# Block 0 of a decoder layer: gates and branch outputs with features on the partitions, and a last projection of split parts

## The chip, the cores and the metric

The kernel runs on one core of a Trainium2 chip. A core has five engines that run their own instruction streams and meet at semaphores: TensorE (PE in the profile; its weight loads are listed as PEld), VectorE (DVE), ScalarE (ACT), GpSimd (POOL) and SyncE (SP, which here issues most transfers). A matmul has a stationary operand, loaded into the array by a weight load (at most 128 x 128), and a moving operand whose columns stream through; its result goes to a bank of PSUM, from which DVE and ACT read.

The metric is the device time of one execution in microseconds. Lower is better.

## What is computed

One decoder layer over 512 tokens with 1024 features. A normalised input goes through one wide projection, three token mixers use parts of it, and each mixer's output is projected, weighted by a gate of its own for every channel, and summed. The sum goes through one more projection and is added to the input. A retrieval layer of 16384 single-neuron experts follows.

```python
h = rmsnorm(x, norm1_g[l])
z = h @ w_in[l]
...
gates = jax.nn.sigmoid((gl + b_gate[l]).astype(jnp.float32)).astype(x.dtype)
gates = gates.reshape(B, S, N_BRANCH, D)
merged = (gates[:, :, 0] * (o_fox @ w_fox_o[l])
          + gates[:, :, 1] * (o_swa @ w_swa_o[l])
          + gates[:, :, 2] * (o_mem @ w_mem_o[l]))
x = x + merged @ w_out[l]
x = x + peer_ffn(rmsnorm(x, norm2_g[l]), w_peer_q[l], peer_keys1[l], peer_keys2[l],
                 peer_u[l], peer_v[l])
```

The change touches the lines from `gates` to `x + merged @ w_out`, for the first 128 tokens only.

## The kernel before

The 512 tokens are four blocks of 128. `GROUPS` (L25) makes two groups of them: block 0 alone, and blocks 1 to 3 together. `mixers(g, hT)` (L623) runs for block 0, then for the other three. When block 0 is through, the search for its experts (`beside`, L904) is emitted in small pieces between the work of the second group; later stages treat the experts of all blocks.

**Split parts.** Most products are made of three. A 32-bit number is split into a high part, rounded to the type that the profile calls fp32r, and the low rest. `mm3` (L143) adds high x high, high x low and low x high into one bank. A weight matrix arrives by DMA in a `raw` tile of 512 KB; `load` (L115) casts it to `whi` on ACT, and `rest` (L122) subtracts to get `wlo`, for block 0 on DVE. There are three slots each for `whi` and `wlo`, and for `raw` three and, during block 0, five more. A few products are made of plain 32-bit numbers in one matmul instruction, for which the trace lists two passes, each with its own weight load.

**Two orientations.** With tokens on the partitions, the block's activations stand in the array and 256 columns of weights move (`gemm_nat`, L283). With features on the partitions, 128 x 128 pieces of weights stand and the group's tokens move (`gemm_tr`, L322): 384 columns for the second group.

**Block 0's gates** (`gates`, L581; called once for each mixer). For each of four pairs of 128-feature chunks, `gemm_nat` makes a [128 tokens, 256 features] result with 24 products. A gate's bias then differs along the columns, so ACT spreads the pair's bias values into a diagonal matrix each (L588), and a plain product of a matrix of ones with them (L300) adds the bias to every token. ACT's tanh (L591) writes a `g` tile; there are `KC` = 8 slots of these. The second group takes `gemm_tr` (L594): there the bias is one number for each partition and goes into the tanh instruction.

**Branch outputs** (`branch`, L599). For each of the four 256-column groups of a mixer's output projection, 12 products of split parts; DVE multiplies by gate + 1 and adds to `merged` (L602, L604, L605). Block 0's `merged` has tokens on its partitions.

**Last projection** (from L651). The projection needs features on the partitions, so block 0's `merged` is turned by eight transposes on PE (L656) and copied with the factor 0.5 by ACT (L658). `gemm_plain` (L303) multiplies it by raw, unsplit weights (L315), four times 8 products of 256 columns. DVE adds the input x (L673), which SP has loaded into freed `g` slots (L670), and ACT takes squares for the next norm (L209). The second group's `merged` has features on its partitions already; it is split (L661, L662) and goes through `gemm_nat`.

**Order.** In the part up to the second group's search a scheduler sets each engine's order ahead of time, by the program's order, priorities and a model of time; it is fixed in the compiled kernel. Each engine then works strictly in that order. The input rows of the second group are fetched and normalised (`get_x`, L940) among block 0's last gates and branch.

Of the kernel before, what the change touches and what calls it, by code (L numbers as in the profile page):

```python
# [7 lines left out]
F32 = mybir.dt.float32  # L8
F32R = mybir.dt.float32r
# [48 lines left out]
def tile_block(ctx: ExitStack, tc: tile.TileContext, t: dict, out: bass.AP):  # L58
# [15 lines left out]
    def bank(tag):  # L74
        return (mixed if BANKS[tag] == 1 else psum).tile([128, 512], F32, tag=tag, name=tag, bufs=BANKS[tag])
# [171 lines left out]
    for hf in range(2):  # L247
        squares(xg[:, 0, hf * 512:(hf + 1) * 512], xsum[:, 0, hf:hf + 1])
    nc.sync.dma_start(cst[:, 1:], t["c_mats"][:, 1:])
    hT = [chunks(by_k(x)) for x in (ep.tile([128, D], F32R, tag="own", name="own"),  # L250
                                    pp.tile([128, D], F32R, name="ownlo", bufs=1))]
    norm_t([xg[:, 0]], xsum, g1, *hT, tags=("tp", "sc", "tp", "sc", "tg", "acc", "mm", "tp"))

    identb = consts.tile([128, 128], BF16, name="identb")
# [25 lines left out]
        for h in range(8):  # L280
            tc.keep_in_program_order(A.mul(slope[:, h], ident, 2.0 ** -(h + 1)))

    def gemm_nat(lhs, src, n, nb, use, more=None, fetch=None, cast=None):  # L283

        w = [load_split(src[half], 4, n, fetch=fetch, cast=cast) for half in range(2)]
        for b in range(nb):
            ps = bank("mm")[:, :n]
            tok = slice(b * 128, (b + 1) * 128)
            if cast:
                for i, (lt, rt) in enumerate(((0, 0), (0, 1), (1, 0))):  # L290
                    for dc in range(KC):
                        PE.matmul(ps, lhs[lt][dc][:, tok], w[dc // 4][rt][:, dc % 4],
                                  start=i == dc == 0, stop=i == 2 and dc == KC - 1)
                use(b, ps)
                continue
            for dc in range(KC):
                wh, wl = (x[:, dc % 4] for x in w[dc // 4])
                mm3(ps, (lhs[0][dc][:, tok], lhs[1][dc][:, tok]), (wh, wl), dc == 0, dc == KC - 1 and not more)
            if more:
                PE.matmul(ps, ones, more, start=False, stop=True)  # L300
            use(b, ps)

    def gemm_plain(lhs, src, n, use, fetch):  # L303

        ps = bank("mm")[:, :n]
        for half in range(2):
            pump()
            raw = fetch(src[half], 4 * n)
            if len(src[half].shape) == 3:
                w = raw[:, :4 * n].rearrange("p (c k w) -> p k c w", c=src[half].shape[0], k=4)  # L310
            else:
                w = raw[:, :4 * n].rearrange("p (k w) -> p k w", k=4)
            for k in range(4):
                dc = 4 * half + k
                PE.matmul(ps, lhs[dc], w[:, k], start=dc == 0, stop=dc == KC - 1)  # L315
        use(0, ps)

    def halves(two):

        return two[:, :, :512], two[:, :, 512:]  # L320

    def gemm_tr(h, src):  # L322

# [257 lines left out]
    def gates(g, i, hT, ccs=range(4)):  # L581
        gs = []
        for cc in ccs:
            c0 = 8 * i + 2 * cc
            if len(GROUPS[g]) == 1:
                bias = pp.tile([128, 256], F32, tag="sq", name="bias")
                for c in range(2):
                    A.activation(bias[:, c * 128:(c + 1) * 128], ident, AF.Copy, scale=hb[:, c0 + c:c0 + c + 1])  # L588
                gs.append(new_g(256))
                gemm_nat(hT, halves(t["w_tr"][c0:c0 + 2]), 256, 1,  # L590
                         lambda b, ps: A.activation(gs[-1], ps, AF.Tanh, scale=0.5), more=bias)  # L591
                continue
            for c in range(2):
                ps = gemm_tr(hT, t["w_tr"][c0 + c])  # L594
                gs.append(new_g(ps.shape[1]))
# [3 lines left out]
    def branch(grp, i, merged, oT, gs):  # L599
# [6 lines left out]

        for cc in range(4):
            wo = load_split(t["w_o"][4 * i + cc], 4, 256)
            if len(GROUPS[grp]) == 1:
                ps = bank("mm")[:, :256]  # L610
                for kc in range(4):
                    mm3(ps, (oT[0][:, kc, :], oT[1][:, kc, :]), (wo[0][:, kc], wo[1][:, kc]), kc == 0, kc == 3)
                gated(merged[:, cc * 256:(cc + 1) * 256], gs[cc], ps)
                continue
            for c in range(2):
                ps = bank("mm")[:, :oT[0].shape[2]]
                cols = slice(c * 128, c * 128 + 128)
# [5 lines left out]
    def mixers(g, hT):  # L623
# [24 lines left out]
            get_x()  # L648
        branch(g, 2, merged, oT, gs)

        mT = [by_k(ep.tile([128, D], F32, tag="own", name="own"))] if nb == 1 else pair(nb)  # L651
        if nb == 1:
            for q in range(2):
                ps = bank("tp")
                for i in range(4):
                    PE.transpose(ps[:, i * 128:(i + 1) * 128], merged[:, (4 * q + i) * 128:(4 * q + i + 1) * 128], ident)  # L656
                ps, dst = ps.rearrange("p (k s) -> p k s", k=4), slice(4 * q, 4 * q + 4)
                A.activation(mT[0][:, dst], ps, AF.Copy, scale=0.5)  # L658
        else:
            for ct, src in enumerate(chunks(by_k(merged))):  # L660
                A.activation(mT[0][:, ct], src, AF.Copy, scale=0.5)  # L661
                V.scalar_tensor_tensor(mT[1][:, ct], src, 0.5, mT[0][:, ct].bitcast(F32),  # L662
                                       op0=OP.mult, op1=OP.subtract)
        mT = [chunks(x) for x in mT]
        x1, sums = by_token(wide(f"mg{g}", nb)), new_sums(4)
        for c in range(4):
# [6 lines left out]
                V.tensor_add(x1[:, b, cols], xs[b], ps)  # L673
                squares(x1[:, b, cols], sums[:, b, c:c + 1])

            if nb == 1:
                gemm_plain(mT[0], t["w_out"][c], 256, use, load_raw)
            else:
                gemm_nat(mT, t["w_out"][c], 256, nb, use)
        return x1, sums  # L680


# [674 lines left out]
```

## Time and profile before

| What | us |
|---|---|
| median of 3 runs | 1583.12 (1581.81 to 1583.77) |
| the profiled execution, as timed | 1584.12 |
| its span, first to last instruction | 1582.3 |
| block 0's gates, branches and projection, by the timeline | about 73 to 184 |
| of that: bias products (L300), 24 passes, recorded | 7.1 |
| of that: bias copies (L588), 24 on ACT | 8.3 |
| of that: plain products of the last projection (L315), 64 passes, recorded | 14.5 |

How to read the rows that follow. A row of the view by groups has line, engine, operation, the names of output and inputs, shapes and count; then busy time in us and the mean of one in ns; then the idle time just before them and what ended it. A row of the timeline has start and duration in us, engine, line, operation, names, shape and the number of instructions that were merged into the row. A row for one tile has the minimum, median and maximum of the durations in ns. A recorded matmul includes its way through the array, so successive ones overlap: from one start to the next is what a product costs in a stream. A shape such as 128x256 is partitions x columns; the moving operand's columns are what is shown for a matmul.

### The profile page before, as it was taken

How to read it: one execution, taken by the hardware profiler on the slowest of the kernel's cores; microseconds unless marked ns; L12 is line 12 of the kernel's file. 1: busy time of each engine (PE TensorE's matmuls, PEld its weight loads, DVE VectorE, ACT ScalarE, POOL GpSimd, SP SyncE). 2: the span in 40 equal slices, each digit the busy share in tenths (PEclk: the TensorE clock that was granted, in tenths of full speed). 3: DMA queues.
4: the chain of work that ended last, by engine and by line, in shares of the span. 5: the costliest groups of instructions: out<-in, count | busy, mean ns of one | idle time of the engine just before them, and what ended most of it. 6: DMA issues, size and time to landing. Idle time of an engine off the chain costs nothing.

```text
span 1582.3 us, 27174 instructions
## 1 busy us (share of the span) xinstructions
PE 1512.7 (96%) x9458; PEld 1373.8 (87%) x9458; DVE 1422.0 (90%) x2661; ACT 819.9 (52%) x1831; POOL 789.2 (50%) x643
## 2 busy tenths in 40 slices
PE   8999899999999989999998999899999999999998
PEld 7989899998898989898787898688888888888887
DVE  6678487888999999999899999799999999999997
ACT  7778336646345533452215998554454454444442
POOL 1100015767576456977444665445555554555451
PEclk9999999999999999999999999999999999999999
DMA  8677657898998899987798999999999999999995
GB/s 319 212 252 251 236 197 251 307 368 310 326 348 309 280 342 337 321 307 250 240 401 303 375 396 386 347 399 390 408 409 409 410 410 407 408 406 404 408 409 193
DMA packets 178361, 531.90 MB, mean 336 GB/s; under 512 B 17456, under 2 KB 46384, under 8 KB 178224
## 3 DMA queue, kind: packets, MB, share of 16 engines
q0 software_dynamic: 73728, 268.47, 44.9%
q1 hardware_dynamic: 94416, 225.95, 39.3%
q10 hardware_dynamic: 10080, 35.75, 5.7%
q8 instruction: 74, 1.21, 0.3%
q14 instruction: 63, 0.52, 0.1%
HBM read 515.42 MB, written 14.68 MB: 335 GB/s over the span
## 4 chain that ended last, share of the span: by engine, by line
PE 58%; DVE 14%; issue 10%; DMA 10%; POOL 5%; ACT 2%; POOLq 0%; SPq 0%; DVEq 0%; ACTq 0%
PE mm L1029 9%; PE mm L146 9%; PE mm L145 9%; PE mm L147 9%; DMA row<-in_peer_v_dram,eidx 6%; POOL row L868 5%; PE sc L1104 3%; DVE two L896 2%; DVE wlo L131 2%; DMA row<-in_peer_u_dram,eidx 2%; PE sc L147 2%; PE sc L146 2%; PE tp L145 2%; PE tp L146 2%; PE sc L145 2%
## 5 line engine op out<-in xcount | busy, mean ns | idle before, releaser
L868 POOL DMA_INDIRECT row<-in_peer_v_dram,eidx x256 | 328.9, 1285 | 289.2 <-DVE two L896 164.1
L868 POOL DMA_INDIRECT row<-in_peer_u_dram,eidx x256 | 316.9, 1238 | 236.3 <-DVE scr L883 115.4
L131 DVE TENSOR_TENSOR wlo<-raw,whi 128x1024 fp32r<-128x1024 f32 (+1 forms) x228 | 278.1, 1221 | 34.2 <-ACT whi L119 30.0
L896 DVE SCALAR_TENSOR_TENSOR two<-row,acts,two 128x1024 f32<-128x1024 f32 x189 | 242.5, 1283 | 4.1 <-DMA row<-in_peer_v_dram,eidx 1.9
L119 ACT CAST whi<-raw 128x1024 fp32r<-128x1024 f32 x146 | 152.6, 1050 | 105.6 <-PE mm L146 59.7
L883 DVE SCALAR_TENSOR_TENSOR scr<-row,own 128x1024 bf16<-128x1024 f32 x128 | 156.2, 1220 | 19.0 <-DMA row<-in_peer_u_dram,eidx 17.9
L883 DVE SCALAR_TENSOR_TENSOR scr<-row,two 128x1024 bf16<-128x1024 f32 x116 | 140.9, 1215 | 5.1 <-DMA row<-in_peer_u_dram,eidx 4.3
L203 POOL TENSOR_TENSOR rsy<-rsv,mhalf 128x4 f32<-128x4 f32 (+5 forms) x25 | 38.6, 1546 | 185.6 <-DVE rsv L202 184.2
L1157 ACT CAST ah<-ga 128x256 fp32r<-128x256 f32 x116 | 47.0, 407 | 158.1 <-PE tp L146 123.8
L147 PE MATMUL mm<-hhi,wlo 128*128 128x384 f32 x320 | 110.6, 346 | 4.5 <-POOL wlo L129 4.5
L145 PE MATMUL mm<-hhi,whi 128*128 128x384 f32 x320 | 111.5, 348 | 1.6 <-ACT hhi L237 1.2
L146 PE MATMUL mm<-hlo,whi 128*128 128x384 f32 x320 | 111.9, 350 | 0.0
L1159 ACT CAST whi<-raw 128x1024 fp32r<-128x1024 f32 x96 | 100.3, 1047 | 16.1 <-DMA raw<-in_peer_v_dram 11.4
L146 PE MATMUL sc<-wlo,ah 128*128 128x512 f32 x256 | 101.2, 395 | 6.3 <-DVE wlo L131 6.3
L145 PE MATMUL mm<-whi,hhi 128*128 128x256 f32 (+1 forms) x360 | 103.7, 290 | 2.9 <-DVE g L604 1.9
L146 PE MATMUL mm<-wlo,hhi 128*128 128x256 f32 (+1 forms) x360 | 102.6, 286 | 1.5 <-DVE wlo L131 1.5
L147 PE MATMUL mm<-whi,hlo 128*128 128x256 f32 (+1 forms) x360 | 101.9, 285 | 0.8 <-DVE hlo L662 0.8
L147 PE MATMUL sc<-whi,al 128*128 128x512 f32 x256 | 101.6, 397 | 0.0
L145 PE MATMUL tp<-whi,ah 128*128 128x512 f32 x256 | 101.0, 395 | 0.0
L145 PE MATMUL sc<-whi,ah 128*128 128x512 f32 x256 | 101.0, 395 | 0.0
L146 PE MATMUL tp<-wlo,ah 128*128 128x512 f32 x256 | 100.9, 394 | 0.0
L147 PE MATMUL tp<-whi,al 128*128 128x512 f32 x256 | 100.6, 393 | 0.0
(323 smaller groups left out, 4527.8 us busy)
## 6 DMA issues: line engine op xcount, KB each, us to landing
raw<-in_peer_v_dram SPq DMA_DIRECT2D x96, 512.0 KB
hhi<-in_uT_dram ACTq DMA_DIRECT2D x68, 512.0 KB
raw<-in_w_tr_dram SPq DMA_DIRECT2D x48, 512.0 KB
raw<-in_w_nat_dram SPq DMA_DIRECT2D x40, 512.0 KB
last<-in_peer_v_dram SPq DMA_DIRECT2D x32, 512.0 KB
hhi<-in_uT_dram SPq DMA_DIRECT2D x26, 512.0 KB
raw<-in_w_o_dram SPq DMA_DIRECT2D x24, 512.0 KB
gd<-st SPq DMA_DIRECT2D x24, 512.0 KB
```

What stands on the lines that cost most here:

```text
L119: (cast or A.copy)(hi[:, :n * w], raw[:, :n * w])
L131: V.tensor_sub(lo, raw, hi.bitcast(F32))
L145: PE.matmul(ps, lh, rh, start=first, stop=False)
L146: PE.matmul(ps, lh, rl, start=False, stop=False)
L147: PE.matmul(ps, ll, rh, start=False, stop=last)
L868: G.indirect_dma_start(out=r, out_offset=None, in_=t["peer_" + tab], in_offset=bass.IndirectOffsetOnAxis(ap=eidx[b][:, j:j + 1], axis=0))
L883: V.scalar_tensor_tensor(scr, r, 1.0, two[0] if b else h2n[b], op0=OP.mult, op1=OP.mult, accum_out=acts[b][:, c]))
L896: V.scalar_tensor_tensor(two[0], r, acts[b][:, c], two[0], op0=OP.mult, op1=OP.add))
L1029: PE.matmul(ps[:, :TD], w[:, dc], h2f[dc], start=dc == 0, stop=dc == KC - 1)
L1104: PE.matmul(ps[:, u], o[:, 1, u], o[:, 0, u], start=True, stop=True)
L1157: A.copy(ah, a)
L1159: A.copy(hi, raw)
```

## The change

For block 0, the gates and the branch outputs take the way that the second group takes.

- `gates` calls `gemm_tr` for every 128-feature chunk: weights stand, block 0's 128 tokens move. The bias goes into the tanh. The bias copies, the product with ones and the parameter `more` are gone.
- `branch` makes two results of 128 features with 12 products each from a loaded piece of weights, and two sets of DVE operations.
- `merged` then has features on the partitions; the transposes are gone. Each of its eight chunks is copied with 0.5 by ACT into the high part and subtracted on DVE for the low part. The low part takes the tile that held the low part of block 0's input (`ownlo`).
- The last projection calls `gemm_nat`: its weights are split like all others (eight casts on ACT, eight subtractions on DVE), with 24 products for each 256 columns. `gemm_plain` and `halves` are gone.

```diff
-                                    pp.tile([128, D], F32R, name="ownlo", bufs=1))]
+                                    pp.tile([128, D], F32R, tag="ownlo", name="ownlo", bufs=1))]
...
-    def gemm_nat(lhs, src, n, nb, use, more=None, fetch=None, cast=None):
+    def gemm_nat(lhs, src, n, nb, use, fetch=None, cast=None):
...
-                mm3(ps, (lhs[0][dc][:, tok], lhs[1][dc][:, tok]), (wh, wl), dc == 0, dc == KC - 1 and not more)
-            if more:
-                PE.matmul(ps, ones, more, start=False, stop=True)
+                mm3(ps, (lhs[0][dc][:, tok], lhs[1][dc][:, tok]), (wh, wl), dc == 0, dc == KC - 1)
             use(b, ps)
-
-    def gemm_plain(lhs, src, n, use, fetch):
...
-    def halves(two):
...
             c0 = 8 * i + 2 * cc
-            if len(GROUPS[g]) == 1:
-                bias = pp.tile([128, 256], F32, tag="sq", name="bias")
-                for c in range(2):
-                    A.activation(bias[:, c * 128:(c + 1) * 128], ident, AF.Copy, scale=hb[:, c0 + c:c0 + c + 1])
-                gs.append(new_g(256))
-                gemm_nat(hT, halves(t["w_tr"][c0:c0 + 2]), 256, 1,
-                         lambda b, ps: A.activation(gs[-1], ps, AF.Tanh, scale=0.5), more=bias)
-                continue
             for c in range(2):
                 ps = gemm_tr(hT, t["w_tr"][c0 + c])
...
             wo = load_split(t["w_o"][4 * i + cc], 4, 256)
-            if len(GROUPS[grp]) == 1:
-                ps = bank("mm")[:, :256]
-                for kc in range(4):
-                    mm3(ps, (oT[0][:, kc, :], oT[1][:, kc, :]), (wo[0][:, kc], wo[1][:, kc]), kc == 0, kc == 3)
-                gated(merged[:, cc * 256:(cc + 1) * 256], gs[cc], ps)
-                continue
             for c in range(2):
                 ps = bank("mm")[:, :oT[0].shape[2]]
...
-        mT = [by_k(ep.tile([128, D], F32, tag="own", name="own"))] if nb == 1 else pair(nb)
-        if nb == 1:
-            for q in range(2):
-                ps = bank("tp")
-                for i in range(4):
-                    PE.transpose(ps[:, i * 128:(i + 1) * 128], merged[:, (4 * q + i) * 128:(4 * q + i + 1) * 128], ident)
-                ps, dst = ps.rearrange("p (k s) -> p k s", k=4), slice(4 * q, 4 * q + 4)
-                A.activation(mT[0][:, dst], ps, AF.Copy, scale=0.5)
-        else:
-            for ct, src in enumerate(chunks(by_k(merged))):
-                A.activation(mT[0][:, ct], src, AF.Copy, scale=0.5)
-                V.scalar_tensor_tensor(mT[1][:, ct], src, 0.5, mT[0][:, ct].bitcast(F32),
-                                       op0=OP.mult, op1=OP.subtract)
+        mT = pair(nb) if nb > 1 else [by_k(ep.tile([128, D], F32R, tag="own", name="own")),
+                                      by_k(pp.tile([128, D], F32R, tag="ownlo", name="ownlo", bufs=1))]
+        for ct, src in enumerate(chunks(by_k(merged))):
+            A.activation(mT[0][:, ct], src, AF.Copy, scale=0.5)
+            V.scalar_tensor_tensor(mT[1][:, ct], src, 0.5, mT[0][:, ct].bitcast(F32),
+                                   op0=OP.mult, op1=OP.subtract)
...
-            if nb == 1:
-                gemm_plain(mT[0], t["w_out"][c], 256, use, load_raw)
-            else:
-                gemm_nat(mT, t["w_out"][c], 256, nb, use)
+            gemm_nat(mT, t["w_out"][c], 256, nb, use)
```

More of the change, by code (lines that the diff above doesn't have):

```diff
@@ L297, in gemm_nat @@
                 wh, wl = (x[:, dc % 4] for x in w[dc // 4])
-                mm3(ps, (lhs[0][dc][:, tok], lhs[1][dc][:, tok]), (wh, wl), dc == 0, dc == KC - 1 and not more)
-            if more:
-                PE.matmul(ps, ones, more, start=False, stop=True)
+                mm3(ps, (lhs[0][dc][:, tok], lhs[1][dc][:, tok]), (wh, wl), dc == 0, dc == KC - 1)
             use(b, ps)
-    def gemm_plain(lhs, src, n, use, fetch):
[L305 to L310, printed above, removed]
-            else:
[L312 to L316, printed above, removed]
-    def halves(two):
-        return two[:, :, :512], two[:, :, 512:]
     def gemm_tr(h, src):
@@ L674, in use @@
                 squares(x1[:, b, cols], sums[:, b, c:c + 1])
-            if nb == 1:
-                gemm_plain(mT[0], t["w_out"][c], 256, use, load_raw)
-            else:
-                gemm_nat(mT, t["w_out"][c], 256, nb, use)
+            gemm_nat(mT, t["w_out"][c], 256, nb, use)
         return x1, sums
```

## The prediction

> **What bounds the kernel now.** I read the page's first and fourth parts, then the busy time by stretch, then the order of time on PE in the part that the change touches. The page first: PE is the busiest engine and has most of the chain that ended last.
>
> ```profile
> PE 1512.7 (96%) x9458; PEld 1373.8 (87%) x9458; DVE 1422.0 (90%) x2661; ACT 819.9 (52%) x1831; POOL 789.2 (50%) x643
> ...
> PE 58%; DVE 14%; issue 10%; DMA 10%; POOL 5%; ACT 2%; POOLq 0%; SPq 0%; DVEq 0%; ACTq 0%
> ```
>
> All that changes belongs to block 0: its gates, its branch outputs and its last projection. By the timeline they lie between 73 and 184 us. The view by stretch (us, busy of PE, PEld, DVE, ACT, POOL with instruction counts, granted clock, DMA share, GB/s) says:
>
> ```profile
> 73.00:100.00 27.00, 24.71 (x204) 23.68 (x203) 20.58 (x33) 22.64 (x49) 6.05 (x4) 1.00 0.83 290
> 100.00:133.00 33.00, 32.60 (x252) 30.04 (x251) 25.95 (x46) 26.20 (x59) 0.69 (x1) 1.00 0.73 239
> 133.00:166.60 33.60, 33.60 (x277) 33.06 (x276) 28.32 (x44) 24.34 (x45) 1.51 (x2) 1.00 0.81 251
> 166.60:183.60 17.00, 15.85 (x80) 13.57 (x79) 2.51 (x6) 3.23 (x10) 0.00 (x0) 1.00 0.52 180
> 183.60:563.00 379.40, 365.87 (x2544) 340.71 (x2543) 333.51 (x757) 193.17 (x484) 218.42 (x190) 0.99 0.85 300
> ```
>
> From 73 to 166.6 us PE is idle 2.7 of 93.6 us; DVE is busy 74.9, ACT 73.2, and DMA has about a fifth free. The granted clock is 1.00 (the 2.4 GHz level). So **PE is the bound here**, and what its instructions gain or lose shows in full, unless DVE catches up. A recorded matmul overlaps its neighbours, so I price PE by steps from start to start, not by durations. Between 166.6 and 183.6 us (the last projection) PE works alone. Behind it PE stays busy 366 of 379 us, and the choice of experts for block 0 waits for this result, so I see no later slack that swallows a shift: what block 0 costs more, the end comes later.
>
> **What a step on PE costs.** From the timeline of PE: first and last of 14 successive products of split parts with 256 columns, then of 18 with 384, then of 9 with 512.
>
> ```profile
> 161.25 0.28 PE L146 MATMUL mm<-wlo,ohi 128*128 128x256 f32 x1
> ...
> 162.78 0.28 PE L147 MATMUL mm<-whi,olo 128*128 128x256 f32 x1
> 308.24 0.34 PE L146 MATMUL mm<-hlo,whi 128*128 128x384 f32 x1
> ...
> 311.23 0.34 PE L145 MATMUL mm<-hhi,whi 128*128 128x384 f32 x1
> 1302.14 0.39 PE L145 MATMUL sc<-whi,ah 128*128 128x512 f32 x1
> ...
> 1304.00 0.39 PE L147 MATMUL tp<-whi,al 128*128 128x512 f32 x1
> ```
>
> The steps are 1.53/13 = 0.118 us, 2.99/17 = 0.176 and 1.86/8 = 0.232: some 0.057 us for every 128 columns. Continued to 128 columns that would be 0.060 us. The change makes the products of gates and branch outputs 128 columns wide (one block's tokens move, weights stand), and twice as many. **No row here shows a split product with 128 columns**, so its step has to be bounded. The nearest rows are plain 32-bit ones: 128 columns (each product is two passes with a load each, and the 16 are passes), 64 columns, and their weight loads.
>
> ```profile
> 191.16 1.95 PE L746 MATMUL mm<-aT,raw 128*128 128x128 f32 x16
> 277.21 1.00 PE L502 MATMUL acc<-v,pT 128*128 128x64 f32 x8
> L146 PEld LDWEIGHTS mm<-wlo,hhi 128*128 128x128 f32 x360 | 68.6, 191 | 3.7 <-issue 1.9 <-DVE wlo L131 1.7
> L502 PEld LDWEIGHTS acc<-v,pT 128*128 128x128 f32 x160 | 20.4, 191 | 1.7 <-issue 1.1 <-ACT p L499 0.3 <-ACT qn L352 0.2
> L373 PEld LDWEIGHTS tp<-cst,p 128*128 128x128 f32 x168 | 20.6, 145 | 2.5 <-issue 1.3 <-ACT p L499 0.3
> ```
>
> A pass with 128 columns steps at (1.95 − 0.28)/15 = 0.112 us. A pass with 64 columns steps at (1.00 − 0.28)/7 = 0.104, though it has half the columns to move. So the columns don't set that step; the load before each pass does. A split product's load is recorded as 191 ns, just as long as the plain pass's 191, while a transpose's takes 145: loads of split parts look like those of plain numbers. With 256 columns the load hides under 0.118 us; with 128 it wouldn't. I take **0.112 us**. Bounds: 0.060 (the line, loads hidden) below, 0.224 (a plain 128-column product, two passes) above.
>
> The Trainium skill (TensorE: Matmul & The Clock Gate, Back-to-back issue gap) gives 81 ns for each load-and-matmul pair at 128 columns in a sustained stream, and 131 ns at 512; by its 81 ns the forecast would be about 1594 us. This trace has 232 ns at 512 columns, so it doesn't bear that pair of figures out for these numbers.
>
> **The change part by part.**
>
> *Gates* (12 pairs of chunks). Before: 24 products of 256 columns and one plain bias product, in two passes, per pair.
>
> ```profile
> 157.40 0.59 PE L300 MATMUL mm<-bias,cst 128*128 128x256 f32 x2
> 157.84 1.05 PE L236 MATMUL sc<-dg,mg 128*128 128x128 f32 x8
> L588 ACT ACTIVATE bias<-cst,hb 128x128 f32<-128x128 f32 x24 | 8.3, 400 | 0.0
> L591 ACT ACTIVATE g<-mm 128x256 f32<-128x256 f32 x12 | 4.6, 381 | 0.0
> ```
>
> The bias passes take 157.84 − 157.40 = 0.44 us a pair. So 288 × 0.118 + 12 × 0.44 = 39.2 us now. After: 576 × 0.112 = 64.5. That is **+25.3 us**. ACT loses the 24 bias copies (8.3 us) and writes 24 narrow gates in place of 12; it isn't the bound. The loads keep their number and size (24 of 512 KB), and the rows that SP fetches only get longer.
>
> *Branch outputs* (12 pairs). 144 × 0.118 = 16.9 us becomes 288 × 0.112 = 32.3: **+15.4 us**. DVE's multiply-adds go from one of 256 columns to two of 128:
>
> ```profile
> L131 DVE TENSOR_TENSOR wlo<-raw,whi 128x1024 fp32r<-128x1024 f32 x43 | 52.4, 1223 | 12.9 <-ACT whi L119 12.8
> L605 DVE TENSOR_TENSOR mg<-mg,g 128x256 f32<-128x256 f32 x7 | 2.9, 420 | 0.1
> L604 DVE SCALAR_TENSOR_TENSOR g<-g,mm 128x256 f32<-128x256 f32 x7 | 2.9, 418 | 0.2 <-PE mm L147 0.2
> L239 DVE SCALAR_TENSOR_TENSOR ownlo<-tp,gcol,own x3: 342/343/344, 10.5 to 15.0; 128x128 fp32r<-128x128 f32 x3
> ```
>
> By the 128-column row (0.343 us) two of them cost 0.69 for 0.42. For branches 0 and 1 that lies under PE's 2.69 us a pair (DVE needs 1.22 + 1.37 there). In branch 2 the split of the merged result comes in as well (a third 0.343 a chunk): DVE needs 1.22 + 6 × 0.343 = 3.28 a pair against PE's 2.69, so 4 × 0.59 = **+2.4 us** may show.
>
> *Last projection.* Removed: the transposes, two copies, and 64 plain passes; added: 96 split products and, on each of the 8 loads, a cast on ACT and a subtraction on DVE.
>
> ```profile
> 166.50 0.28 PE L147 MATMUL mm<-whi,olo 128*128 128x256 f32 x1
> ...
> 179.54 3.62 PE L315 MATMUL mm<-raw,own 128*128 128x256 f32 x16
> 183.20 0.42 DVE L673 TENSOR_TENSOR mg<-g,mm 128x256 f32<-128x256 f32 x1 [3.25 <-PE mm L315]
> L119 ACT CAST whi<-raw 128x1024 fp32r<-128x1024 f32 x42 | 43.7, 1049 | 12.7 <-PE mm L147 8.4 <-issue 1.6 <-ACT pT L375 1.0
> ```
>
> From the last branch product to the last addition it takes 183.62 − 166.50 = 17.1 us now; the plain passes are 64 × (3.62 − 0.38)/15 = 13.8 of them. After: 96 × 0.118 = 11.3, a matmul's end and an addition (0.7), and about 1 us until the last chunk is split; most of that wait lies under the products of the chunks before it. Together 13.0: **−4.1 us**. Per group of 256 columns DVE needs 2 × 1.22 + 0.42 = 2.87 us and ACT 2 × 1.05 + 0.42, against 24 × 0.118 = 2.83 on PE: they keep pace, since three slots let loads be split ahead. Without that cover the last projection would be some 2 us longer.
>
> *Waits.* A slower PE gives loads time to be split in advance; of the 2.7 us idle I take back **−1**. The gates' eight slots now hold one set instead of two. Here that adds no wait: in program order each set's readers come before the next set is written. The transfers of x into freed slots stand on SP's queue ahead of later weights; the first slots come free a quarter of the way through branch 2, some 8 us before the projection by the steps above.
>
> Sum: 25.3 + 15.4 + 2.4 − 4.1 − 1.0 = **+38.0 us**. The profiled execution took 1584.1 us (span 1582.3), the median is 1583.1, 1.0 less: 1622.1 as profiled, **1621.1 us** as measured.
>
> **Rivals.**
>
> *Loads hide even at 128 columns* (step 0.060): gates 34.6 for 39.2, branches 17.3 for 16.9, projection −4.1; DVE would then be the bound of branch 2 and give back 3 us or so. About −5: 1578 us, **faster**. It decides below a step of 0.068 us, where 864 steps equal the 56.1 us removed from gates and branches plus the rest. For it: the straight line through three widths. Against it: the 64-column passes.
>
> *Loads hide half* (0.086): 864 × 0.026 = 22.5 less than the forecast, 1599 us. For it: loads and products overlap at every width in the trace (PEld busy 87%, PE 96%). Against it: the 64-column row (0.104 where a pure load would be 0.112) leaves little room. The 81 ns of the Trainium skill's section named above would be a case of this rival.
>
> *Narrow split products lose their single pass* (0.224): 864 × 0.112 = 96.8 more, 1718 us. For it: every split product in the trace has 256 columns or more. Against it: nothing in the steps of 256, 384 and 512 hints at a change of rate.
>
> *New waits on top of the forecast*: DVE runs 0.343 us pieces between 1.22 us subtractions, and PE's two result banks wait behind them; at 0.3 us for each of 48 banks of gates and branches, +14: 1635 us.
>
> That the change doesn't do what it says is hardly open: the loops fix the number of products, and the loads are repeated for equal weights already (the three products have equal counts of loads).
>
> **How the numbers follow.** Chances: forecast 70% (about 1609 to 1633), new waits 9%, half hidden 6%, two passes 8%, all hidden 5%, and 2% for steps so near 0.068 that nothing shows. The range 1598 to 1648 takes in the first three and leaves out 15%. Faster by over 0.2% (about what a measurement of this kernel can tell from no change) 0.05, within it 0.02, slower 0.93.
>
> **What would show it.** Right: products of 128 columns (weights first, own second) starting 0.11 us apart; PE without idle time from 73 to about 205 us; block 0's last addition near 222 us for 183.2; all later stretches shifted by that and not changed. Wrong: steps of 0.06 or 0.22 us; DVE busy throughout with PE waiting for it in branch 2; or a later stretch that becomes shorter by what block 0 lost.

## The result and the profile after

| | before | after |
|---|---|---|
| median, both kernels timed together, 6 runs each | 1583.44 us (1581.81 to 1588.44) | **1604.32 us** (1600.91 to 1606.94) |
| ratio to before | | **1.0142**, 95% interval 1.0122 to 1.0162 |
| the profiled execution, as timed | 1584.12 | 1604.52 |
| its span | 1582.3 | 1602.8 |

The kernel became slower by 20.9 us. Direction and range were forecast (1598 to 1648), the size was not: 38.0 us were. The page of after, first part:

```profile
PE 1542.5 (96%) x9890; PEld 1410.6 (88%) x9890; DVE 1433.3 (89%) x2697; ACT 825.3 (51%) x1831; POOL 784.6 (49%) x643
```

PE is busy for 30 us more (1512.7 before), while the span grew by 20.5. So the work came, and somewhere some 10 us were taken back. The view by stretch of after, over the times that the prediction showed for before (us; busy of PE, PEld, DVE, ACT, POOL; granted clock, DMA share, GB/s):

```profile
73.00:100.00 27.00, 27.00 (x244) 26.95 (x244) 15.11 (x21) 17.18 (x35) 1.83 (x1) 1.00 0.66 199
100.00:133.00 33.00, 33.00 (x281) 31.05 (x279) 20.77 (x45) 18.10 (x44) 2.01 (x2) 1.00 0.58 186
133.00:183.60 50.60, 50.60 (x446) 50.29 (x444) 32.29 (x51) 30.28 (x53) 3.21 (x3) 1.00 0.60 188
```

PE is never idle here, and PEld is nearly as busy as PE. DMA fell to about 0.6 from 0.7 to 0.8. Next, a list of what PE waited for, from 73 us to the end of block 0; columns are the total in us, times, the longest. Before (six lines, 3.9 us together, two of them shown) and after (its only line):

```profile
PE tg L366 <- DVE qn L348: 1.2, 1, 1.2
PE mm L315 <- ACT own L658: 1.2, 2, 0.7
```

```profile
PE mm L146 <- DVE wlo L131: 0.2, 1, 0.2
```

The timeline of PE in after, in branch 2: the first and last of 23 successive products of 128 columns, then the last branch product and the first of the last projection; and of DVE, block 0's last addition:

```profile
189.94 0.28 PE L147 MATMUL mm<-ohi,wlo 128*128 128x128 f32 x1
...
192.40 0.28 PE L145 MATMUL mm<-ohi,whi 128*128 128x128 f32 x1
...
200.87 0.27 PE L147 MATMUL mm<-ohi,wlo 128*128 128x128 f32 x1
201.17 0.36 PE L145 MATMUL mm<-whi,own 128*128 128x256 f32 x1
```

```profile
213.64 0.42 DVE L631 TENSOR_TENSOR mg<-g,mm 128x256 f32<-128x256 f32 x1 [1.64 <-PE mm L147]
```

The step is 2.46/22 = **0.112 us**, as taken. Block 0 ends at 213.64 + 0.42 = 214.1 us, for 183.6 before: 30.4 later, where 38.0 were forecast. A part of that difference is an accident of the two profiled executions: up to block 0's first gate product the programs are the same, but that product starts at 72.1 us in before and at 70.4 in after. Before has 6.8 us at half clock ahead of it, after 3.4. Counted from the first gate product to the last addition, block 0 takes 111.1 us before and 143.3 after: the change costs **32.2 us** there. The second group keeps that shift: its last addition before and after stands at

```profile
633.06 0.41 DVE L673 TENSOR_TENSOR mg<-g,mm 128x256 f32<-128x256 f32 x1
```

```profile
663.71 0.41 DVE L631 TENSOR_TENSOR mg<-g,mm 128x256 f32<-128x256 f32 x1
```

30.7 us later. What follows is the second group's search for experts, which ends with the Exps of its gate weights. I call the time from that addition to the start of the last Exp **the search**. The timeline of ACT at its end, before and then after:

```profile
759.53 1.28 ACT L784 ACT_TABLE_LOAD   x1 [6.83 <-DVE ex L781]
760.83 0.40 ACT L784 ACTIVATE ex<-ex,rstd 128x128 f32<-128x128 f32 x1
761.25 1.28 ACT L1031 ACT_TABLE_LOAD   x1
762.54 0.38 ACT L1031 ACTIVATE ga<-mm 128x256 f32<-128x256 f32 x1
762.94 1.28 ACT L784 ACT_TABLE_LOAD   x1
764.24 0.69 ACT L784 ACTIVATE ex<-ex,rstd 128x128 f32<-128x128 f32 x2
```

```profile
783.71 1.28 ACT L739 ACT_TABLE_LOAD   x1 [7.77 <-DVE ex L736]
785.00 0.98 ACT L739 ACTIVATE ex<-ex,rstd 128x128 f32<-128x128 f32 x3
```

In before the scheduler put a Gelu (L1031) between the three Exps, so the function table was loaded three times up to the last of them; in after the Exps are together and it is loaded once. The last of three Exps merged into one row starts at 785.6 in after, at 764.5 in before: the shift is 21.1 us now, and the search lasts **131.5 us before and 121.9 after**. Behind it the time to the end of the span is the same within 1 us (817.5 and 816.9 from the last Exp's start). So of the missing 17 us 7.6 went in block 0, 1.7 of them by its earlier start, and 9.6 in the search.

For the search there is a second difference. The view by groups of the search, DVE, counts the expert rows of block 0 that were accumulated in it (busy time in us, mean in ns); the groups of the gathers' line up to the start of the search show how many such rows had been fetched by then (minimum, median and maximum in ns, first and last start in us). Before, then after:

```profile
L890 DVE SCALAR_TENSOR_TENSOR mg<-row,acts,mg 128x1024 f32<-128x1024 f32 x11 | 22.8, 2073 | 0.0
```

```profile
L868 POOL DMA_INDIRECT row<-in_peer_v_dram,eidx x49: 942/1020/3093, 513.8 to 632.9; - x49
```

```profile
L845 DVE SCALAR_TENSOR_TENSOR mg<-row,acts,mg 128x1024 f32<-128x1024 f32 x8 | 14.3, 1782 | 0.1
```

```profile
L823 POOL DMA_INDIRECT row<-in_peer_v_dram,eidx x52: 944/1020/3092, 542.2 to 663.6; - x52
```

After has 52 rows gathered by the start of the search and 8 accumulations left, before 49 and 11. DVE is the busy engine there (view by stretch of the search, before and after): 123.1 of 131 us, then 115.1 of 121.6.

```profile
633.50:764.50 131.00, 121.43 (x673) 115.04 (x674) 123.09 (x616) 51.09 (x85) 102.05 (x91) 0.96 0.82 292
```

```profile
664.00:785.60 121.60, 116.33 (x667) 111.45 (x667) 115.07 (x614) 47.86 (x82) 97.50 (x88) 0.99 0.82 295
```

### The profile page after: what moved, and what is told of

Same layout as the page of the kernel before. It is cut to its first block, busy times and chain, and to the rows that moved or that the text cites. A ratio compares the mean times of both kernels' runs of the same rounds, so it can differ in the third digit from the quotient of the medians.

```text
span 1602.8 us, 28089 instructions
## 1 busy us (share of the span) xinstructions
PE 1542.5 (96%) x9890; PEld 1410.6 (88%) x9890; DVE 1433.3 (89%) x2697; ACT 825.3 (51%) x1831; POOL 784.6 (49%) x643
## 3 DMA queue, kind: packets, MB, share of 16 engines
q8 instruction: 78, 1.28, 0.3%
## 4 chain that ended last, share of the span: by engine, by line
PE 58%; DVE 14%; DMA 12%; issue 8%; POOL 4%; ACT 3%; DVEq 0%; POOLq 0%; ACTq 0%
PE mm L984 9%; PE mm L147 9%; PE mm L146 9%; PE mm L145 9%; DMA row<-in_peer_u_dram,eidx 4%; DMA row<-in_peer_v_dram,eidx 4%; POOL row L823 4%; PE sc L1059 3%; DVE two L851 3%; PE sc L146 2%; PE sc L147 2%; PE sc L145 2%; PE tp L145 2%; PE tp L146 2%; PE tp L147 2%
## 5 line engine op out<-in xcount | busy, mean ns | idle before, releaser
L823 POOL DMA_INDIRECT row<-in_peer_u_dram,eidx x256 | 313.3, 1224 | 238.9 <-DVE scr L838 134.4
L131 DVE TENSOR_TENSOR wlo<-raw,whi 128x1024 fp32r<-128x1024 f32 (+1 forms) x236 | 288.1, 1222 | 55.6 <-ACT whi L119 52.7
L119 ACT CAST whi<-raw 128x1024 fp32r<-128x1024 f32 (+1 forms) x154 | 160.7, 1048 | 126.7 <-PE mm L146 80.8
L1114 ACT CAST whi<-raw 128x1024 fp32r<-128x1024 f32 x96 | 100.3, 1047 | 9.5 <-DMA raw<-in_peer_v_dram 7.3
```

What stands on the lines that cost most here:

```text
L119: (cast or A.copy)(hi[:, :n * w], raw[:, :n * w])
L131: V.tensor_sub(lo, raw, hi.bitcast(F32))
L823: G.indirect_dma_start(out=r, out_offset=None, in_=t["peer_" + tab], in_offset=bass.IndirectOffsetOnAxis(ap=eidx[b][:, j:j + 1], axis=0))
L1114: A.copy(hi, raw)
```

## The experiments

Two theories for the 9.6 us stood against each other. **Order**: the scheduler made another order for the second group and the search, by chance of the change, and with another order the 9.6 us would not come back. **Give-back**: the search has slack, and whatever block 0 loses, a third of it comes back there. A third question was the size of the step itself. Each kernel was timed beside the kernel before, whose median was 1579.9 to 1581.8 us in these sets (1583.4 beside the changed kernel); so ratios are compared rather than microseconds. Times inside a kernel are from its profiled execution.

**A long delay in block 0 of the kernel before.** 70 plain products that nobody reads, ahead of the last projection:

```diff
+        if nb == 1:
+            ps = bank("tp")
+            for _ in range(70):
+                PE.matmul(ps[:, :256], mT[0][7], cst[:, 1:3], start=True, stop=True)
```

> The kernel before with 70 plain products (140 passes of 256 columns, 0.222 us each by the rows of the last projection: 31.1 us) whose results nothing reads, set on PE ahead of block 0's last projection. Block 0's last addition should come 31 us later in every theory. Theory 'order' (the 10 us that the change got back behind block 0 come from another order that the planner chose for the second group and the search): what comes back is this kernel's own luck, anything from -10 to +10 us, so 1593 to 1625 us with no rule. Theory 'give-back' (the search has slack that swallows a third of any delay of block 0): about 31 - 10 = +21 us, 1604 us, with the return between the second group's last addition and the last gate weights.

Measured: 1611.31 us, ratio 1.0181 (1.0152 to 1.0210). Block 0's last addition came 28.3 us later, the second group's 28.1, the last Exp 28.1, and the search lasted 131.5 us as in the kernel before. A delay nearly as long as the change's was not repaid up to the end of the search. Give-back falls, as a rule for any delay.

**A short delay**, in the same place:

```diff
-            for _ in range(70):
+            for _ in range(20):
```

> The same with 20 plain products: 40 x 0.222 = 8.9 us on PE ahead of block 0's last projection. Theory 'order': block 0 ends 9 us later, and the stretch behind it is longer or shorter by up to 10 us with no relation to the delay: 1582 to 1602 us. Theory 'give-back': a third comes back, about +6 us, 1589 us.

Measured: 1585.53 us, ratio 1.0026 (1.0005 to 1.0047). Block 0's last addition 4.9 us later, the last Exp 4.5, the search 129.0 us. Of the 9 us expected 8.6 are there when counted from the first gate product, 119.7 us for 111.1; but that product starts 3.7 us earlier than in before, in an execution without half clock up to there.

**Another order, with next to nothing changed.** At the start of the program PE makes `UNREAD` = 36 bf16 products that nobody reads, 6.7 us in all, while it waits for the first loads. Four more of them make the scheduler lay out another order further on. In the kernel before:

```diff
-UNREAD = 36
+UNREAD = 40
```

> The kernel before with 40 instead of 36 unread products at the very start, where PE waits for the first transfer: less than 1 us of work. Theory 'order': the planner sees other times and makes another order for most of the part that it plans, so the time moves by some us either way (a shift of 3 us or more, with block 0's end or the search's length moved) although nothing was added. Theory 'give-back': no change, 1583 +- 2 us, and block 0's end and the search's length as before within 1 us.

Measured: 1583.44 us, ratio 1.0015 (0.9998 to 1.0033); block 0's last addition 0.3 us later, search 129.0. The order moved, but the time did not by the 3 us that Order expected: the second group became 3.0 us longer and the search 2.5 shorter. The same edit in the changed kernel:

> The changed kernel with 40 instead of 36 unread products at the start. Theory 'order': the 10 us that came back behind block 0 are not kept as they are; the stretch from the second group's last addition to the end changes by several us, 1598 to 1620 us. Theory 'give-back': 1604 +- 2 us, with the same return behind block 0.

Measured: **1618.08 us**, ratio 1.0220 (1.0197 to 1.0243) for the changed kernel's 1.0142, some 12 us more. Block 0's last addition stands 32.2 us later than before, the last Exp 35.5, and the search is back at 131.5. Its ACT timeline and its DVE group in the search are those of the kernel before:

```profile
794.99 1.28 ACT L739 ACT_TABLE_LOAD   x1 [8.04 <-DVE ex L736]
796.28 0.40 ACT L739 ACTIVATE ex<-ex,rstd 128x128 f32<-128x128 f32 x1
796.70 1.28 ACT L986 ACT_TABLE_LOAD   x1
798.00 0.38 ACT L986 ACTIVATE ga<-mm 128x256 f32<-128x256 f32 x1
798.40 1.28 ACT L739 ACT_TABLE_LOAD   x1
```

```profile
L845 DVE SCALAR_TENSOR_TENSOR mg<-row,acts,mg 128x1024 f32<-128x1024 f32 x11 | 22.7, 2060 | 0.4 <-issue 0.3
```

A Gelu between the Exps again, and 11 accumulations again. Against the profile of after, the search is 9.6 us longer, the second group 3.1, and the first gate product 1.7 later (72.1 us, as in before). The changed layout thus costs some 34.8 us in this order (0.0220 of 1581.8) and 20.9 in the other.

**A third order of the changed kernel:**

```diff
-UNREAD = 36
+UNREAD = 32
```

> The changed kernel with the planner's count of unread banks at 32 in place of 36: nothing of the work changes, another order of block 0's followers comes out. Theory 'order': block 0's last addition within 3 us of the changed kernel's 213.6, and an end that falls anywhere between about 1595 and 1622, with the difference to the changed kernel made after block 0 and mostly in the search stretch (121.9 us there). Rival 'the changed layout itself gives the search 10 us': search 120 to 124 us and 1601 to 1608, as in the changed kernel; then the run with 40 would be the odd one.

Measured: 1605.52 us (1602.21 to 1612.66, 5 runs), ratio 1.0159 (1.0140 to 1.0177); block 0's last addition at 212.9, search 129.0 with 50 rows gathered by its start and 10 accumulations in it. The rival that the layout itself makes the search short expected 120 to 124 us: it falls by the search, though the time lies in its span. The profiled execution is the slowest of the five, 7 us above the median, at a granted clock of 0.986; the three from 1602.2 to 1605.5 us have 0.993. So where the median's 1605.5 comes from can't be read from this profile; that stays open.

**The Exps together, in program order.** The kernel before, with the three Exps kept in the program's order:

```diff
-            A.activation(bf, bf, AF.Exp, scale=rstd[:, GROUPS[g][b]:GROUPS[g][b] + 1])
+            tc.keep_in_program_order(A.activation(bf, bf, AF.Exp, scale=rstd[:, GROUPS[g][b]:GROUPS[g][b] + 1]))
```

> The kernel before with the three exponentials of the second group's gate weights kept together on ACT, so that no Gelu comes between them; the orders of DVE, PE, POOL and SP are those of the kernel before. If two table loads (1.28 us each) and the waiting Gelu are a third of the 10 us that the changed kernel got back, the stretch from the second group's last addition to the last exponential falls from 131.5 us to about 128.3, and the time by 3 us to about 1579. If the loads lie beside other work, the time stays within 1 us.

Measured: 1608.52 us, ratio 1.0191 (1.0167 to 1.0214): a miss. The Exps are together, but behind 11 more Gelus, each of which waits for its product on PE; the first and the last of 12 such Gelus that follow each other at 3.45 us, and the Exps behind them:

```profile
749.94 0.38 ACT L1031 ACTIVATE ga<-mm 128x256 f32<-128x256 f32 x1 [3.07 <-PE mm L1029]
...
787.93 0.38 ACT L1031 ACTIVATE ga<-mm 128x256 f32<-128x256 f32 x1 [3.07 <-PE mm L1029]
788.33 1.28 ACT L784 ACT_TABLE_LOAD   x1
789.63 0.98 ACT L784 ACTIVATE ex<-ex,rstd 128x128 f32<-128x128 f32 x3
```

The search lasts 159.5 us and all behind it comes 22 to 26 us later. ACT is half idle over the span, yet its order here sets the end.

**The Exps together, ahead of the Gelus**, by a priority that puts them ahead of the remaining Gelus. On the other engines the order is that of the kernel before, instruction by instruction, but for one neighbouring pair on DVE:

```diff
-            A.activation(bf, bf, AF.Exp, scale=rstd[:, GROUPS[g][b]:GROUPS[g][b] + 1])
+            with tc.high_priority(LATER) if g else ExitStack():
+                A.activation(bf, bf, AF.Exp, scale=rstd[:, GROUPS[g][b]:GROUPS[g][b] + 1])
```

> The kernel before, with one thing changed: the three Exps of the second group's gate weights stand one behind the other on ACT, ahead of the remaining Gelus, so two reloads of the function table are gone. The orders of PE, DVE, POOL and SP are the same as in the kernel before, instruction by instruction. Theory 'order' (the 10 us that the search got back in the changed kernel have two parts: 3.3 us of table reloads with a Gelu between the Exps, and some 6 us of another order of rows and dense work): search stretch 131.5 to about 128, spread of the second group and end 3 us earlier, 1578 to 1581. Rival 'reloads are covered' (something else holds the gate weights, and the reloads lie beside it): search 131.5, end unchanged. Rival 'the reloads are the whole of it': search near 122, end 10 us earlier, 1573.

Measured: 1577.32 us, ratio 0.9985 (0.9972 to 0.9998); search **128.4 us**, 3.1 shorter. The same in the changed kernel with 40 unread products:

> The changed kernel with 40 in place of 36 as the count of unread banks (measured 1618.1 with a search of 131.5 us and a Gelu between the Exps), and in it the three Exps one behind the other; the orders of PE, DVE, POOL and SP stay as in that run, instruction by instruction. Theory 'order': search near 128, end some 3 us earlier than that run, 1614 to 1616, so that about 10 us of the difference to the changed kernel (1604.3) stay with the order of rows and dense work. Rival 'the reloads are the whole of it': search near 122, end 1605 to 1608. Rival 'covered': 1618, unchanged.

Measured: 1614.34 us, ratio 1.0219 (1.0195 to 1.0242); search **128.4 us**, 3.1 shorter than in that kernel without the edit (800.0 to 795.8 for the last Exp). The reloads are worth 3.1 us of the search, alike in both layouts, and are not the whole of it. In the whole time the second pair doesn't show them: the ratios with and without are equal (1.0220 and 1.0219).

**What sets the rest of the search.** POOL issues the gathers. In the fourteen profiles of all kernels its instructions come in just four orders, I to IV, and DVE's in the search in the same four. Rows are the gathers of the second kind issued by the start of the search, from the view by groups of each trace; the second group is the time between block 0's last addition and its own. The kernel with the Exps in program order has order I too; it is left out, since Gelus hold its Exps up.

| order | kernel | rows by then | Exps | second group, us | search, us |
|---|---|---|---|---|---|
| I | before; 70 products; changed with 40 unread | 49 | apart | 449.9, 449.7, 453.2 | 131.5, 131.5, 131.5 |
| I | before, Exps first; changed with 40, Exps first | 49 | together | 448.7, 454.9 | 128.4, 128.4 |
| II | 20 products; before with 40; split projection alone; changed with 32 | 50 | apart | 452.0, 452.8, 454.7, 453.6 | 129.0, 129.0, 129.0, 129.0 |
| III | bias on DVE alone; changed with four streams (below) | 50 | together | 452.4, 445.5 | 127.0, 127.1 |
| IV | **after**; bias on DVE and split projection | 52 | together | 450.1, 456.2 | 121.9, 121.8 |

Each order stands in both layouts, and with the Exps alike the search is equally long in both, to 0.1 us. So the order sets the search, and the layout does not. Neither does TensorE's clock: 131.5 us stand at a granted clock of 0.96 (before) and 0.98 (changed with 40 unread), 129.0 at 0.96 to 0.99.

What in an order does it is less sure. A row more ahead of the search goes with 2.5 us less in it (131.5 to 129.0), three rows with 6.5 (128.4 to 121.9); one accumulation takes 2.07 us of DVE in the row above. With the 3.1 us of the reloads that is the 9.6 us, but the shares don't simply add: with 50 rows the Exps together are worth 2.0 us (129.0 to 127.0). The reloads were switched by themselves; the rows were not, they came with whole orders. That they are the cause is read from the levels and from DVE's rows.

A shorter search is not yet a shorter kernel. In the old layout the second group became longer as the search became shorter, by 2.1 to 4.8 us in order II and by 6.3 in order IV. In after it did not (450.1 us for 449.9), so there the 9.6 us remain. The search's order doesn't set the second group: 450.1 and 456.2 us stand under order IV, 452.4 and 445.5 under order III. What sets it, and whether the new layout has a part in that, stays open.

**The parts of the change.** The kernel before with the split last projection only, its transposes kept:

```diff
                 A.activation(mT[0][:, dst], ps, AF.Copy, scale=0.5)
+                V.scalar_tensor_tensor(mT[1][:, dst], ps, 0.5, mT[0][:, dst].bitcast(F32),
+                                       op0=OP.mult, op1=OP.subtract)
...
-                gemm_plain(mT[0], t["w_out"][c], 256, use, load_raw)
+                gemm_nat(mT, t["w_out"][c], 256, nb, use)
```

> The kernel before with the last projection alone changed: the transposes stay, their result is split into two parts, the weights are split, and 96 split products take the place of the 64 plain passes. Gates and branch outputs as before. By the prediction's terms block 0 ends 13.8 - 11.3 = 2.5 us earlier, less up to 1 us for the wait on the split of the second half. Theory 'order': the search is 122 to 132 us long as the planner's order falls out, so the time is anything from 1571 to 1584 us. Rival: eight more casts and subtractions hold PE up and block 0 ends later than before.

Measured: 1584.30 us, ratio 1.0027 (1.0012 to 1.0042). No gain: PE waits for the copies and splits behind the transposes (list of waits on PE, 165 to 190 us; three of its four lines):

```profile
PE mm L145 <- ACT own L659: 2.8, 2, 1.4
PE mm L147 <- DVE ownlo L660: 0.6, 1, 0.6
PE mm L146 <- DVE wlo L131: 0.5, 1, 0.5
```

Block 0's last addition came 6.3 us later, not earlier. These 3.9 us eat what the cheaper products save; about 5 us more, by my estimate, are the profiled execution's own: from the first gate product on it has 10.2 us at half clock (a granted 0.66 over 100 to 110 us and 0.93 over 165 to 190), where before has none, and it is 8 us above the median. In the change the chunks are split one by one beside the branch products; I take that cover for what makes its projection shorter, but no run took the cover away alone.

**The bias without a product, in the old layout.** The bias comes as a row by DMA to all partitions, and DVE adds it before the tanh; once with the split projection and once alone:

```diff
-                for c in range(2):
-                    A.activation(bias[:, c * 128:(c + 1) * 128], ident, AF.Copy, scale=hb[:, c0 + c:c0 + c + 1])
+                nc.sync.dma_start(bias, bass.AP(tensor=row.tensor, offset=row.offset + 128 * c0, ap=[[0, 128], [1, 256]]))
...
+                def use(b, ps):
+                    V.tensor_add(gs[-1], ps, bias)
+                    A.activation(gs[-1], gs[-1], AF.Tanh, scale=0.5)
```

> The kernel before with tokens on the partitions kept, the projection split as in the run before, and the gates' bias added by DVE from a row that a transfer spreads over the partitions: the 24 passes of the bias products and the 24 bias copies go, 12 additions of 0.42 us come on DVE, and 12 small transfers. Prediction's terms: 12 x 0.43 = 5.2 us on PE for the bias and 2.5 for the projection, so block 0 ends up to 7.7 us earlier, less what waits for loads and DVE take back (half of it, if PE then waits for DVE and ACT as the kernel before did): 3 to 8 us. With the exponentials together, as they are in this order, 3 more: 1572 to 1578 us. Slower than before if DVE has become the bound of the gates.

> The kernel before with its layout and its plain last projection; of the gates only the bias product goes: the bias comes as a row by DMA to all partitions and DVE adds it to each result before the Tanh. By the steps of the kernel before, 12 x 0.44 = 5.3 us less on PE, 12 x 0.42 = 5.0 us more on DVE, which in the gates is busy three quarters of the time. If PE's steps decide block 0: its last addition near 178 us, against 183.2. If DVE takes over as the limit there: 181 to 184. Theory 'order' says that what the end does follows from that and from the order that the list makes of the search: Exps behind one another in this order (3.3 us) plus -6 to +6 us for the rows, so 1570 to 1580. Rival 'the gain of the run with bias row and split projection came from the projection': no gain here, 1580 to 1584.

Measured: 1571.34 us, ratio 0.9948 (0.9931 to 0.9965), with the split projection; **1570.33 us, ratio 0.9944 (0.9929 to 0.9960)**, without. Both beat the kernel before and the changed one, and the whole time doesn't tell them apart. Alone, block 0's last addition stands at 173.7 us, 9.5 ahead of before. Of that 3.2 us are the start: this profile has the clock at 1.00 in the first 30 us, where that of before has 0.89, and its first gate product stands at 68.9 us for 72.1. From there block 0 takes 104.7 us for 111.1, 6.3 less, where the bias passes are 5.3. With the split projection it takes 110.0: in this layout the split projection made block 0 longer, by 5.3 us. Its search is 5.2 us shorter, its second group 3.8 longer.

**The step by itself.** In the changed kernel, four streams of 48 products of split parts ahead of the last projection, with other widths of the moving and the standing operand:

```diff
+            for n, m in ((256, 128), (128, 128), (64, 128), (128, 64)):
+                for _ in range(48):
+                    PE.matmul(ps[:m, :n], mT[0][:, 0, :m], mT[0].rearrange("p k s -> p (k s)")[:, :n],
+                              start=True, stop=True)
```

> The changed kernel with four streams of 48 products of rounded numbers (results unread) ahead of block 0's last projection: 256 columns with 128 stationary, 128 with 128, 64 with 128, and 128 with only 64 stationary columns. Theory 'load' (at 128 columns the step is the weight load of 128 columns): steps of 0.118, 0.112, 0.11 and about 0.06 us. Rival 'narrow products stream at half rate': 0.118, 0.112, 0.056 and 0.112 us. Time of the whole is not the question (about 20 us more).

Measured (one execution, 1627.28 us). The products of the last three streams by form, in one stretch each, with minimum, median and maximum of a record in ns, first and last start in us, and the forms (standing 128*128 or 128*64, then moving); below them the view by stretch:

```profile
L626 PE MATMUL tp<-own x48: 224/274/283, 205.4 to 210.6; 128*128 128x128 f32 x47, 128*128 128x256 f32 x1
L626 PE MATMUL tp<-own x22: 243/277/277, 210.7 to 213.0; 128*128 128x64 f32 x21, 128*128 128x128 f32 x1
L626 PE MATMUL tp<-own x20: 401/401/401, 213.9 to 218.0; 128*128 128x64 f32 x20
L626 PE MATMUL tp<-own x46: 308/308/347, 218.4 to 223.2; 128*64 128x128 f32 x46
```

```profile
205.60:210.60 5.00, 5.00 (x48) 5.00 (x46) 0.45 (x2) 0.00 (x0) 0.00 (x0) 1.00 0.00 0
210.90:213.20 2.30, 2.30 (x23) 2.30 (x23) 0.00 (x0) 0.00 (x0) 0.00 (x0) 1.00 0.02 7
214.20:218.20 4.00, 4.00 (x21) 4.00 (x20) 0.00 (x0) 0.00 (x0) 0.00 (x0) 0.50 0.00 0
218.60:223.40 4.80, 4.80 (x47) 4.80 (x47) 0.00 (x0) 0.00 (x0) 0.00 (x0) 0.50 0.00 0
```

128 moving columns: 5.2/47 = 0.111 us. 64 moving columns: 2.3/21 = 0.110, nothing saved. Then the granted clock fell to 0.50 (the 1.2 GHz level) after PE had worked without a gap through the streams, and 64 moving columns cost 4.1/19 = 0.216. At that same clock the products with 64 *standing* columns, though 128 move, cost 4.8/45 = 0.107: half. (Either operand may set this 0.107; what it shows is that the 0.216 is not the moving side's.) Up to 128 moving columns, the standing operand's columns, so the load, set the step.

## Why the prediction was right and wrong

**Right: the step.** Products of 128 columns start 0.112 us apart. From the first gate product to block 0's last addition PE's steps grew by 38.3 us (sum over all starts in both traces, without what a distance has over the median step of its form: 99.6 to 137.9), against terms of 25.3, 15.4 and −4.1, together 36.6. The reason, that the load sets the step at 128 columns, was taken from the plain 64-column passes (0.72/7 is 0.103 us, not the 0.104 written there), and the streams show it. The rivals with 0.060, 0.086 and 0.224 fall. In the first stretch of after's gates PEld is busy 26.95 of 27.00 us: the loads overlap the products, but they follow each other without a gap. The 81 ns of the Trainium skill (TensorE: Matmul & The Clock Gate, Back-to-back issue gap) is not borne out for split products: no stream of them here stepped faster than 0.110 us with a load of 128 columns at either clock.

**Right: the projection.** From the last branch product to the last addition 214.06 − 200.87 = 13.2 us; 13.0 were forecast.

**Too high: DVE in branch 2, +2.4.** It was worked out with 0.343 us an instruction. The narrow multiplications of branches 1 and 2 in after, by form (minimum, median, maximum in ns):

```profile
L575 DVE SCALAR_TENSOR_TENSOR g<-g,mm x16: 276/282/290, 148.9 to 201.2; 128x128 f32<-128x128 f32 x16
```

They took 0.28. What all branch products together waited, by the same count, is 1.7 us in after and was 2.2 in before. The term is nil.

**Mis-sized: the idle time taken back, −1.0.** This is the step that failed within block 0: from the first gate product on, the waits, which are what that sum left out, fell by 6.1 us (11.4 to 5.3). About 1 us of that stands in the projection's −4.1 already. So +38.3 became the +32.2, and with the first gate product 1.7 us earlier the +30.4 that the traces show. The four profiles of the changed layout without the streams (36, 40 twice and 32 unread products) all take 143.2 to 143.3 us from the first gate product on, so the 32.2 us are no luck; the 1.7 us are. I had read idle time from busy sums and found 2.7 us up to 166.6; that count left out the projection's own waits and all waits too short to show, because a record of 0.28 us covers a gap behind a step of 0.12. The list of waits on PE from 73 us on fell by 3.7 us (3.9 to 0.2); the rest is short gaps.

**Wrong: no later slack, later stretches unchanged.** The prediction's own sign of being wrong, a later stretch that becomes shorter, came true in the search: 9.6 us. But slack was not the reason. A pure delay of 28.3 us was still 28.1 us at the last Exp and 28.6 in the whole time (0.0181 of 1581.8), and the same changed kernel in another order kept all of its 32 us through the search. The scheduler had laid out the second group and the search anew: three rows of block 0's experts more were done ahead of the search, the second group became no longer by it (450.1 us for 449.9), and the Exps came out together. What I priced was near for one order; with 40 unread products the same change measures 34.8 us, 3 below the forecast. Both 1604 and 1618 us lie in the range; which of them came is the luck of the order. Another order of the second group was no rival of mine, though a scheduler that sees every edit makes it. Why it chose order IV with 36 unread products and not with 40 stays open.

**Of the other signs:** PE without idle time in the gates and branches came true; DVE as the bound of branch 2 and the new waits at the narrow results' banks didn't come (the list of waits on PE has one line, 0.2 us).

## What to carry to other kernels

A split product costs its weight load when few columns move: swap the operands so that the wide side moves, and count products before turning a layout for the sake of a bias or a few transposes; here the bias was worth some 5 us and had a cheaper way (a row added on DVE, 0.9944).

Where a scheduler lays out the order, an edit changes stages that it doesn't touch. Make a neutral edit of both kernels beside the real one: here it moved the changed kernel by some 12 us (ratios 1.0142 and 1.0220) and the kernel before by 2, which is as much as many a change is worth. Then compare the orders themselves: four orders and the place of the Exps explained the search of all fourteen profiles.

Read waits from starts, not from busy sums, on an engine whose records overlap; and count a stage from its own first instruction, so that what the start of an execution lost or won stays out.

## What was not expected of the hardware

- Up to 128 moving columns the step of a split product follows the standing operand's columns: 0.111 us for 128 moving and 0.110 for 64 moving columns; at the 0.50 clock 0.216 with 128 standing and 64 moving, 0.107 with 64 standing and 128 moving.
- A change of function table cost its load, 1.28 us, and nothing else to be seen: the Exp starts 0.02 us after the load's end (759.53 + 1.28, then 760.83). The Trainium skill (ScalarE: Activation LUTs, What ACT_TABLE_LOAD costs) adds a drain of about 1.38 us to each; these rows have no place for it, and taking two loads and a Gelu out from between the Exps gave 3.1 us.
- Executions of one program on one chip lay up to 10 us apart (1602.2 to 1612.7 in five of the kernel with 32 unread products), and the profiled ones have stretches at the half clock in different places: 0.89 over the first 30 us in before, 1.00 with the bias on DVE alone.
